# Moving the matmul operands of four stages to other byte addresses in SBUF

## The chip, the core and the metric

The kernel runs on one core of one Trainium2 chip (trn2). The metric is the device time of one execution in microseconds. Three runs of the kernel before gave 2288.55, 2289.33 and 2289.89 us; their median is 2289.33 us. The profile is one further execution, which took 2291.27 us; the span of its instructions is 2289.5 us.

## The reference

One encoder layer is applied to a prompt of 2048 tokens and to 8 sample streams of 16 tokens each (16 tiles of 128 prompt tokens, and one tile of sample tokens). Everything is float32, with a model width of 1024:

```python
qm, km, vm, om, ip, fp, qa, ka, va = split_in(x @ w_in)          # 1024 -> 2824
hm = mlstm_chunkwise(qm, km, vm, logi, logf, C0, n0, m0)          # 4 heads x 128, chunk 64
hm = sigmoid(om) * head_norm(hm)
ha = swa(rope(qa), rope(ka), va, attn_sinks)                      # window 128, 8 q / 2 kv heads x 64
h  = layer_norm(ALPHA * x + concat(hm, ha) @ w_out)               # 1024 -> 1024
u  = h @ w_up                                                     # 1024 -> 2 x 2816
a, g = split(b_conv + causal_conv3(u, w_conv))
y  = layer_norm(ALPHA * h + (silu(g) * a) @ w_down)               # 2816 -> 1024
```

The outputs are y for prompt and samples, the mLSTM states, the last keys and values and the last two rows of u.

## The kernel before

**Four dense stages.** The input projection, the output projection, the up projection and the down projection hold nearly all of the TensorE work. Input, up and down projection use Strassen's scheme: seven products of half-size blocks (numbered 1 to 7 in the code) take the place of eight. The attention and mLSTM work of small matmuls (`Chains`) is woven between the matmuls of the input and output projections.

**Each float32 product is three matmuls.** `split` (L219 to L222) makes of each operand a high part, cast to `float32r` on ScalarE, and a low part, the difference, on VectorE. A product is then high by high, high by low and low by high. The high and low parts stand in SBUF buffers of 1024 or 1536 elements per partition.

**Stationary and moving operand.** A matmul has a stationary operand of 128 columns, which a weight load (LDWEIGHTS, row `PEld` of the profile) brings into the array, and a moving operand of 128 to 512 columns that streams through it (row `PE`). In the profile a matmul is written out<-in, with the moving operand's name first: `dps<-oh,w` streams tokens `oh` against weights `w`, `dps<-w,oh` streams weights against tokens. The load for the next matmul begins when the matmul before it begins to stream, so that in an unbroken run the two read SBUF at the same time.

**Which operand moves.** In the input projection (`i_product`, L721) the model's weights `w` are stationary for the groups g = 0 and 1 and the tokens move, with 256 columns; for g = 2 to 4 it is the other way round. The gates and keys (`i_direct`, L747) stream 264 columns of weights. The output projection (`mm3`, L226 to L228) streams 512 columns of weights against 128 tokens. The up projection (`f_product`, L1895) streams 384 tokens (in the last block of tokens 320) against 128 columns of weights `uw`. The down projection (`product` in `f_downs`, L2103) streams 512 columns of weights `uw` against 128 tokens `fu`.

**Buffers and addresses.** Pools give out their buffers one after the other, from the left or the right end of SBUF. `pad` (L216) takes a buffer of n bytes that nobody uses, to shift what follows. All weight buffers of a pool have one tag with 4 buffers each (`wlo`, `whi`, in `half` and `f_slot`), and two more (`wex`) in the pools `wx1sb` and `wx2sb`. They are 4096 bytes per partition for weights (4352 for the gates), whole multiples of 256, so that every buffer of a stage starts at the same address modulo 256. The token buffers `hh` and `hl` of the up projection come from `f_buf`, which in the pool `fsb` adds 64 elements, so that the down projection can reuse them as `fu` with an offset of 56 elements.

**What sets the order.** TensorE's order is written out by hand; each other engine and DMA queue runs its instructions in the order in which the code records them. Semaphores between engines are derived from reads, writes and buffer reuse.

Of the kernel before, what the change touches and what calls it, by code (L numbers as in the profile page):

```python
# [8 lines left out]
F32 = mybir.dt.float32  # L9
# [5 lines left out]
P = 128  # L15
# [20 lines left out]

WB = 4
WR = 7


IBLOCKS = [[0, 1, 2, 3, 16], [4, 5, 6, 7], [8, 9, 10, 11], [12, 13, 14, 15]]
# [164 lines left out]
class Prog:  # L206
# [23 lines left out]
    def run(self):  # L230
        PS = bass.MemoryType.PSUM
        nb = len(OBLOCKS)
        with ExitStack() as es:
            def enter(*a, **k):
                cm = self.pool(*a, **k)
                return cm.__enter__(), cm
            close = lambda cm: cm.__exit__(None, None, None)
            self.cp = es.enter_context(self.pool("const"))
            self.dp = es.enter_context(self.pool("dram", space=bass.MemoryType.DRAM))
            es.enter_context(self.tc.manual_schedule(engines={mybir.EngineType.PE}))  # L240
            self.setup()
# [12 lines left out]
            wx, wxcm = enter("wx1sb")  # L254
            self.pad(wx, 192)
            self.unit_more(wx)
            self.mp, mcm = enter("osb")
            self.o_setup()
            for b in range(nb - 1):
                chains.weave(self.late_done(self.o_block(b)))  # L260
            chains.until(NPT - 1)
            chains.drain()
            close(tpcm)
            close(tcm)
            self.fp, fcm = enter("fsb", side="right")
            self.fup, fpcm = enter("fup", 3, PS)
            self.f_setup()
            dense = self.o_block(nb - 1)
            first = self.f_hT(0)
            next(first)  # L270
            n = 0
            for i, _ in enumerate(dense):
                if i >= 2:
                    next(first, None)

                if i in (4, 7, 10):
                    self.f_tokens(0, *{4: (1,), 7: ("t1",), 10: ("t3", 7, "t2", 6)}[i])
# [12 lines left out]
            self.pad(self.wx, 192)  # L290
            self.f2, f2cm = enter("f2sb")
            self.pad(self.f2, 64)
            self.f3, f3cm = enter("f3sb")
            self.pad(self.f3, 192)
            self.pad(self.fp, 224)
            self.f_ups(n)
            close(f3cm)
            close(f2cm)
            self.f2, f2cm = enter("d2sb")
            self.f3, f3cm = enter("d3sb")  # L300
            self.f_downs()
            for cm in (f3cm, f2cm, wxcm, fpcm, fcm):
                close(cm)


    def setup(self):
# [3 lines left out]
        nc.vector.memset(self.eps, EPS)  # L310
        self.mhalf = cp.tile([P, 8], F32, name="mhalf")
        nc.vector.memset(self.mhalf, -0.5)
        self.zqk = [dp.tile([8, P, P * len(b)], F32, name=f"zqk{i}") for i, b in enumerate(IBLOCKS)]
        self.zws = [[dp.tile([1 if g < KEPT else 2, P, 4, HT], F32, name=f"zws{g}_{i}") for i in range(4)] for g in range(NG)]
        self.zo = [[dp.tile([len(b), P, 512], F32, name=f"{n}{i}") for i, b in enumerate(IBLOCKS)] for n in ("zqa", "zog", "zv")]
# [79 lines left out]
    def release(self, n):  # L395
        self.halves[1] += n

    def half(self, shape):
        n = self.halves[0]
        self.halves[0] += 1  # L400
        if self.extra is not None:
            e = (n - self.extra) % (2 * WB + 2)
            if e < 2:
                return self.wx.tile(shape, F32R, name="w", tag="wex", bufs=2)
        self.turn = 1 - self.turn
        return self.wp.tile(shape, F32R, name="w", tag=("wlo", "whi")[self.turn], bufs=WB)

    def unit_more(self, wx):
        self.wx, self.extra = wx, self.halves[0]
# [62 lines left out]
    def next_split(self):  # L472
# [7 lines left out]
        self.us += 1  # L480
        if u[0] == "g":
            e = self.raw_of.pop(u)
            w = self.half([P, 2, 2, 272])[:, :, :, :264]
            self.split(w[:, 0], w[:, 1], e[0])
            e[1] = True
            self.wu[u] = w[:, 0], w[:, 1]
            return True
        hi, lo = self.half([P, 1024]), self.half([P, 1024])
        if self.kept(u):
            for i, t in enumerate((hi, lo)):  # L490
                self.nc.sync.dma_start(t.bitcast(F32), self.zws[u[2]][SUMS.index(u[3])][i].rearrange("p a b -> p (a b)"))
# [1212 lines left out]
    def f_hT(self, b):  # L1704
# [12 lines left out]
        if b == 0:  # L1717
# [1 line left out]

            n = len(tiles) // 2  # L1720
            for ts, tags in ((range(n), ("hh6", "hl6")), (range(n, 2 * n), ("hh7", "hl7"))):
                w = [self.f_buf(fp, F32, "hst", tag, [3, 512]) for tag in tags]
# [31 lines left out]
    def f_tokens(self, b, *steps):  # L1754
# [6 lines left out]
        for s in steps:  # L1761
# [7 lines left out]
                V.tensor_sub(r3, r3, r2)  # L1769
            else:  # L1770
                pool = self.fp if s in (1, 7, 6) else self.f3 if s == 4 else self.f2
                hi, lo = [self.f_buf(pool, F32R, f"{n}{s}", f"{n}{s}", [4, 384]) for n in ("hh", "hl")]
                self.split(hi[:, :, :h], lo[:, :, :h], src[s])
                self.hc[b, s] = hi[:, :, :h], lo[:, :, :h]

    def f_buf(self, pool, dt, name, tag, shape, at=0):

        t = pool.tile([P, 1536 + (64 if pool is self.fp else 0)], dt, name=name, tag=tag, bufs=1)[:, at:at + 1536]
        d = dict(zip("abc", shape[:-1]))
        return t.rearrange(f"p ({' '.join(d)} m) -> p {' '.join(d)} m", **d)  # L1780

    def f_slot(self, dt=F32R):
        self.slot = (self.slot + 1) % 10
        if self.slot < 8:
            return self.wp.tile([P, KD, P], dt, name="uw", tag=("whi", "wlo")[self.slot % 2], bufs=WB)
        return self.wx.tile([P, KD, P], dt, name="uw", tag="wex", bufs=2)

    def f_raw(self, b, j):

# [9 lines left out]
    def f_next(self):  # L1799
# [6 lines left out]
        if s == 1:  # L1806
            if (b, j) not in self.wr:
                self.f_raw(b, j)
            if b == 0:
                v, g = self.wr[b, j]  # L1810
                s12, s34 = self.f_slot(F32), self.f_slot(F32)
# [4 lines left out]
                self.wr[b, j] = v, g, s12, s34  # L1816
        if s == 5 and (b, j) != (len(FBLOCKS) - 1, NFF - 1):
            self.f_raw(b + (j + 1) // NFF, (j + 1) % NFF)
        w = self.f_slot().rearrange("p (i k) m -> p i k m", i=2)
        i = SUMS.index(s) if s in SUMS else None  # L1820
        keep = None if i is None else self.zw[j][i].rearrange("p (i k m) -> p i k m", i=2, k=4)
        if b and i is not None:
# [206 lines left out]
    def d_weights(self):  # L2029
# [17 lines left out]
    def d_tokens(self):  # L2047
# [28 lines left out]
    def f_downs(self):  # L2076
# [13 lines left out]
        nb, nu = len(FBLOCKS), len(DUNITS)  # L2090
        ys, ops = {}, {}
        last_tile = FBLOCKS[-1][0]
        st = self.wp.tile([P, 2, 6], F32, name="st", tag="st", bufs=1)

        def product(s, p, units):
# [124 lines left out]
```

## Time and profile before

| | us |
|---|---|
| median of three runs | 2289.33 |
| the profiled execution | 2291.27 |
| its span, first to last instruction | 2289.5 |
| TensorE busy (PE) | 2269.4 |
| weight loads (PEld) | 2083.6 |
| VectorE busy | 1808.9 |
| ScalarE busy | 1272.9 |

Lines such as L721 are lines of the kernel before. A row of groups shows busy time and the mean duration of one instruction. Matmuls overlap each other at their ends, so the time that one costs is the distance between the starts of two that follow each other, which this document calls the period; it is had from the first and the last start and the count. The views by line give each group's least, median and greatest duration, then first and last start. The chain of waits gives start, length, engine, tile, line and count.

### The profile page before, as it was taken

To read this page: it belongs to the slowest core of one execution; us is meant where nothing else is said; L and a number is where in the kernel's file an instruction comes from. 1 tells how busy PE (TensorE), PEld (TensorE's weight loads), DVE (VectorE), ACT (ScalarE), POOL (GpSimd) and SP (SyncE) were. 2 spreads that over 40 slices of the span, in tenths; PEclk is the share of its full clock that TensorE was granted. 3 is DMA by queue.
4 is the path that set the end of the run, shared out by engine and by line. 5 is a ranking of instruction groups with operands and counts; after the bars stand their busy time and mean duration, and the time that the engine had idled before them with its cause. 6 is when DMAs were issued, how large, how long until landed. Compare 5 with 4: busy or idle time off the path is not lost. (4 is left out here: it accounts for less than half of the span.)

```text
span 2289.5 us, 39775 instructions
## 1 busy us (share of the span) xinstructions
PE 2269.4 (99%) x14293; PEld 2083.6 (91%) x14293; DVE 1808.9 (79%) x3068; ACT 1272.9 (56%) x2373; POOL 275.5 (12%) x509
## 2 busy tenths in 40 slices
PE   8999999999999999999999999999999999999998
PEld 8999999999878778999999999999999988888876
DVE  8787687777688888998778777778766786995987
ACT  5453476776766656555556555555555644444442
POOL 0001001000021110211112000113111200200200
PEclk9999999999999999999999999999999999999999
DMA  7989998899998867898778999988998786757752
GB/s 280 321 313 317 319 317 275 276 308 298 329 315 266 270 217 273 310 328 302 285 272 272 307 305 311 307 269 290 323 288 262 253 291 227 252 164 223 251 157 84
DMA packets 302133, 631.30 MB, mean 276 GB/s; under 512 B 47404, under 2 KB 140656, under 8 KB 301936
## 3 DMA queue, kind: packets, MB, share of 16 engines
q1 hardware_dynamic: 297264, 615.06, 79.5%
q0 software_dynamic: 3520, 10.56, 1.5%
q10 hardware_dynamic: 1152, 3.15, 0.4%
q8 instruction: 113, 1.85, 0.3%
q14 instruction: 84, 0.69, 0.1%
HBM read 457.02 MB, written 171.64 MB: 275 GB/s over the span
## 5 line engine op out<-in xcount | busy, mean ns | idle before, releaser
L1895 PE MATMUL fup<-hh,uw 128*128 128x384 f32 (+1 forms) x1848 | 476.9, 327 | 0.2 <-ACT ub L1924 0.2
L1895 PE MATMUL dps<-hh,uw 128*128 128x384 f32 (+1 forms) x1848 | 476.7, 327 | 0.0
L1895 PEld LDWEIGHTS fup<-hh,uw 128*128 128x128 f32 x1848 | 329.1, 188 | 0.5 <-ACT ub L1924 0.4
L1895 PEld LDWEIGHTS dps<-hh,uw 128*128 128x128 f32 x1848 | 329.1, 188 | 0.0
L1895 PE MATMUL fup<-hl,uw 128*128 128x384 f32 (+1 forms) x924 | 301.9, 327 | 1.0 <-DVE hl L222 1.0
L1895 PE MATMUL dps<-hl,uw 128*128 128x384 f32 (+1 forms) x924 | 301.6, 326 | 0.0
L1953 DVE SCALAR_TENSOR_TENSOR cc<-u,cw,cc 128x768 f32<-128x768 f32 (+1 forms) x264 | 258.0, 978 | 38.6 <-ACT cc L1951 30.2
L221 ACT CAST uw<-wraw 128x1024 fp32r<-128x1024 f32 x126 | 123.6, 981 | 229.0 <-PE dps L2103 122.5
L721 PE MATMUL dps<-w,oh 128*128 128x256 f32 x1344 | 250.3, 282 | 0.4 <-ACT dps L815 0.4
L222 DVE TENSOR_TENSOR w<-wraw,w 128x1024 fp32r<-128x1024 f32 (+2 forms) x163 | 186.1, 1149 | 61.8 <-ACT w L221 60.4
L221 ACT CAST w<-wraw 128x1024 fp32r<-128x1024 f32 (+2 forms) x163 | 160.3, 992 | 112.6 <-PE dps L721 58.3
L721 PEld LDWEIGHTS dps<-w,oh 128*128 128x128 f32 x1344 | 209.5, 188 | 11.5 <-issue 8.1
L222 DVE TENSOR_TENSOR uw<-wraw,uw 128x1024 fp32r<-128x1024 f32 x126 | 142.3, 1129 | 61.7 <-ACT uw L221 61.2
L721 PE MATMUL dps<-w,ol 128*128 128x256 f32 x672 | 186.8, 278 | 0.0
L1895 PEld LDWEIGHTS fup<-hl,uw 128*128 128x128 f32 x924 | 173.6, 188 | 1.7 <-DVE hl L222 1.6
L721 PE MATMUL dps<-oh,w 128*128 128x256 f32 x896 | 170.7, 284 | 3.8 <-DVE w L222 2.2
L2103 PE MATMUL fup<-uw,fu 128*128 128x512 f32 x726 | 173.8, 396 | 0.0
L1895 PEld LDWEIGHTS dps<-hl,uw 128*128 128x128 f32 x924 | 173.6, 188 | 0.0
L2103 PEld LDWEIGHTS fup<-uw,fu 128*128 128x128 f32 x726 | 136.4, 188 | 33.0
L2103 PE MATMUL dps<-uw,fu 128*128 128x512 f32 x660 | 165.0, 396 | 0.0
L2103 PEld LDWEIGHTS dps<-uw,fu 128*128 128x128 f32 x660 | 124.0, 188 | 30.0
L721 PEld LDWEIGHTS dps<-oh,w 128*128 128x128 f32 x896 | 140.5, 188 | 10.1 <-issue 4.1
(320 smaller groups left out, 4565.1 us busy)
## 6 DMA issues: line engine op xcount, KB each, us to landing
uw<-zw SPq DMA_DIRECT2D x176, 512.0 KB, 5.1
zw<-uw SPq DMA_DIRECT2D x88, 512.0 KB, 3.3
w<-zws SPq DMA_DIRECT2D x72, 512.0 KB, 6.3
wv<-wup SPq DMA_DIRECT2D x66, 512.0 KB, 5.4
wraw<-wi SPq DMA_DIRECT2D x65, 512.0 KB, 5.1
wraw<-zt SPq DMA_DIRECT2D x60, 512.0 KB, 4.6
wraw<-wdn SPq DMA_DIRECT2D x45, 512.0 KB, 4.9
wraw<-wo SPq DMA_DIRECT2D x40, 512.0 KB, 4.9
```

Of the source, the lines that this page charges most:

```text
L221: nc.scalar.copy(hi, src)
L222: return nc.vector.tensor_sub(lo, src, hi.bitcast(F32)).ins
L721: mm(o, l, r, start=s in (1, 7) and c == k == i == 0, stop=k == 3 and i == 2, skip_group_check=True)
L1895: mm(ps, l[:, k], r[:, k], start=s in (1, 7) and k == 0 and i == 0, stop=k == 3 and i == 2, skip_group_check=True)
L1953: V.scalar_tensor_tensor(c[:, v], u[:, i:i + n], w[i], c[:, v], op0=ALU.mult, op1=ALU.add)
L2103: mm(ps, l[:, k, c], r[:, k], start=s in (1, 4, 7) and u == 0 and k == 0 and i == 0, stop=u == nu - 1 and k == n - 1 and i == 2, skip_grou ...
```

## The change

It shifts buffers and leaves everything else. The order of the instructions on all five engines and what each waits for are the same in both built programs. All weight buffers become 1088 elements (4352 bytes) long, and `half` and `f_slot` return a slice that begins `at` elements into the buffer. The padding is arranged so that weight buffers begin at 0 modulo 256 in every pool, where they began at 192. `f_buf` with its extra elements is gone.

The table gives, from the built programs, how far the stationary operand of the next load lies from the moving operand of the running matmul, in bytes modulo 256 (called the distance below).

| stage, line before | matmuls | columns | moving | next load of | distance before | after |
|---|---|---|---|---|---|---|
| input, g = 0 and 1, L721 | 1344 | 256 | tokens oh, ol | w | 192 | 64 |
| input, g = 2 to 4, L721 | 2016 | 256 | w | oh, ol | 64 | 64 |
| input, samples, L731 | 240 | 256 | w | xs | 96, 128, 192 | 0 to 224 mixed |
| gates and keys, L747 | 408 | 264 | w | oh, ol | 0, 64, 128, 192 | 0, 64, 128, 192 |
| output, L226 to L228 | 816 | 512 | w | oh, ol | 64 | 0 |
| up, L1895 | 3696 | 384 | hh, hl | uw | 192 | 192 |
| up, last block, L1895 | 1848 | 320 | hh, hl | uw | 192 | 192 |
| down, L2103 | 1980 | 512 | uw | fu | 32 | 0 |

In the gates' row a third of the pairs has a distance of 0 before and after; the rest trades 64, 128 and 192 among each other. The operands of the attention and mLSTM matmuls keep their addresses. Raw weights (`wraw`), residual rows (`yacc`) and the raw tokens of the down projection (`r2` to `r4`) move mostly from 192 to 0 modulo 256 with the rest.

```diff
+WS = 1088
...
             wx, wxcm = enter("wx1sb")
-            self.pad(wx, 192)
...
             self.wx, wxcm = enter("wx2sb")
-            self.pad(self.wx, 192)
             self.f2, f2cm = enter("f2sb")
-            self.pad(self.f2, 64)
...
         nc.vector.memset(self.mhalf, -0.5)
+        self.pad(cp, 64)
...
-    def half(self, shape):
+    def half(self, at, size):
...
-                return self.wx.tile(shape, F32R, name="w", tag="wex", bufs=2)
+                return self.wx.tile([P, WS], F32R, name="w", tag="wex", bufs=2)[:, at:at + size]
         self.turn = 1 - self.turn
-        return self.wp.tile(shape, F32R, name="w", tag=("wlo", "whi")[self.turn], bufs=WB)
+        return self.wp.tile([P, WS], F32R, name="w", tag=("wlo", "whi")[self.turn], bufs=WB)[:, at:at + size]
...
-        hi, lo = self.half([P, 1024]), self.half([P, 1024])
+        at = 0 if u[0] == "o" else 16 if u[2] < 2 else 48
+        hi, lo = self.half(at, 1024), self.half(at, 1024)
...
-                hi, lo = [self.f_buf(pool, F32R, f"{n}{s}", f"{n}{s}", [4, 384]) for n in ("hh", "hl")]
+                hi = pool.tile([P, 4, 384], F32R, name=f"hh{s}", tag=f"hh{s}", bufs=1)
+                lo = pool.tile([P, 4, 384], F32R, name=f"hl{s}", tag=f"hl{s}", bufs=1)
...
-    def f_slot(self, dt=F32R):
+    def f_slot(self, at, dt=F32R):
...
+        return w[:, at:at + D].rearrange("p (k m) -> p k m", k=KD)
...
-        w = self.f_slot().rearrange("p (i k) m -> p i k m", i=2)
+        w = self.f_slot(48).rearrange("p (i k) m -> p i k m", i=2)
...
-        hi, lo = [self.f_slot().rearrange("p a b -> p (a b)") for _ in range(2)]
+        hi, lo = [self.f_slot(0).rearrange("p a b -> p (a b)") for _ in range(2)]
...
-        w = self.f_buf(self.fp, F32R, "fu", ("hh1", "hl1", "hh7", "hl7", "hh6", "hl6")[self.ring % 6], [2, 2, 384], 56)
+        w = self.fp.tile([P, 2, 2, 384], F32R, name="fu", tag=("hh1", "hl1", "hh7", "hl7", "hh6", "hl6")[self.ring % 6], bufs=1)
```

More of the change, by code (lines that the diff above doesn't have):

```diff
@@ L482, in next_split @@
             e = self.raw_of.pop(u)
-            w = self.half([P, 2, 2, 272])[:, :, :, :264]
+            w = self.half(0, WS).rearrange("p (i k m) -> p i k m", i=2, k=2)[:, :, :, :264]
             self.split(w[:, 0], w[:, 1], e[0])
@@ L1721, in f_hT @@
             for ts, tags in ((range(n), ("hh6", "hl6")), (range(n, 2 * n), ("hh7", "hl7"))):
-                w = [self.f_buf(fp, F32, "hst", tag, [3, 512]) for tag in tags]
+                w = [fp.tile([P, 3, 512], F32, name="hst", tag=tag, bufs=1) for tag in tags]
                 for c, t in enumerate(ts):
@@ L1771, in f_tokens @@
                 pool = self.fp if s in (1, 7, 6) else self.f3 if s == 4 else self.f2
-                hi, lo = [self.f_buf(pool, F32R, f"{n}{s}", f"{n}{s}", [4, 384]) for n in ("hh", "hl")]
+                hi = pool.tile([P, 4, 384], F32R, name=f"hh{s}", tag=f"hh{s}", bufs=1)
+                lo = pool.tile([P, 4, 384], F32R, name=f"hl{s}", tag=f"hl{s}", bufs=1)
                 self.split(hi[:, :, :h], lo[:, :, :h], src[s])
                 self.hc[b, s] = hi[:, :, :h], lo[:, :, :h]
[L1776 to L1780, printed above, removed]
-    def f_slot(self, dt=F32R):
+    def f_slot(self, at, dt=F32R):
         self.slot = (self.slot + 1) % 10
         if self.slot < 8:
-            return self.wp.tile([P, KD, P], dt, name="uw", tag=("whi", "wlo")[self.slot % 2], bufs=WB)
-        return self.wx.tile([P, KD, P], dt, name="uw", tag="wex", bufs=2)
+            w = self.wp.tile([P, WS], dt, name="uw", tag=("whi", "wlo")[self.slot % 2], bufs=WB)
+        else:
+            w = self.wx.tile([P, WS], dt, name="uw", tag="wex", bufs=2)
+        return w[:, at:at + D].rearrange("p (k m) -> p k m", k=KD)
     def f_raw(self, b, j):
@@ L1810, in f_next @@
                 v, g = self.wr[b, j]
-                s12, s34 = self.f_slot(F32), self.f_slot(F32)
+                s12, s34 = self.f_slot(48, F32), self.f_slot(48, F32)
                 V.tensor_add(s12[:, :4], g[:, :4], g[:, 4:])
@@ L2092, in f_downs @@
         last_tile = FBLOCKS[-1][0]
+        self.pad(self.wp, 192)
         st = self.wp.tile([P, 2, 6], F32, name="st", tag="st", bufs=1)
```

## The prediction

> **What bounds the kernel now.** I read the page's totals first, then TensorE's waits, then single runs of matmuls.
>
> ```profile
> span 2289.5 us, 39775 instructions
> PE 2269.4 (99%) x14293; PEld 2083.6 (91%) x14293; DVE 1808.9 (79%) x3068; ACT 1272.9 (56%) x2373; POOL 275.5 (12%) x509
> PEclk9999999999999999999999999999999999999999
> ...
> PE dps L721 <- DVE w L222: 2.2, 2, 1.3
> PE dps L336 <- DVE zero L331: 2.0, 1, 2.0
> ```
>
> TensorE is busy for 99% of the span, at the full granted clock in all 40 slices, and the longest of its waits for another engine come to 2.2 and 2.0 us in all. Whatever a matmul's period loses or gains is therefore the kernel's, less what the woven work of other engines takes back. By stage (input, output, up, down projection):
>
> ```profile
> 20.00:614.00 594.00, 587.91 (x5048) 558.88 (x5047) 443.76 (x1008) 361.93 (x792) 43.96 (x70) 1.00 0.91 304
> 615.00:894.00 279.00, 278.11 (x1530) 216.93 (x1529) 238.43 (x556) 174.12 (x418) 44.93 (x49) 1.00 0.81 270
> 894.00:1818.00 924.00, 922.83 (x5636) 921.09 (x5635) 727.25 (x977) 519.95 (x879) 155.36 (x355) 1.00 0.86 293
> 1818.00:2281.00 463.00, 462.83 (x1982) 371.56 (x1980) 380.24 (x488) 203.78 (x260) 30.06 (x30) 1.00 0.63 209
> ```
>
> The columns are stage, length, then busy time and count of PE, PEld, VectorE, ScalarE, GpSimd, then clock and DMA share. VectorE comes nearest to TensorE in the output stage, 238 of 279 us; nowhere is there another engine within a few per cent, so a few us saved on TensorE will reach the end.
>
> Since no instruction changes its place or its waits, the only thing that can change is how long one instruction takes at its new addresses. ScalarE, VectorE and the DMA queues, which also get new addresses, have 15% or more to spare in each stage except for the DMA's 0.91 in the first; I cost them at nothing. Were that cover gone in the first stage, transfers that take 1% longer or shorter would move the end by 594 x 0.91 x 1% = 5 us. So the question is the period of a matmul at each distance. A matmul's recorded length overlaps the next, so periods come from starts.
>
> **512 columns, at 64 and 32.**
>
> ```profile
> L227 PE MATMUL dps<-w,oh x25: 393/398/398, 850.5 to 867.3; 128*128 128x512 f32 x25
> 1818.43 46.20 PE fup L2103 x198
> ```
>
> In the output stage L227 is one in three: 16.8 us over 24 steps is 700 ns for three, a period of 233.3 ns at distance 64. The chain of waits has 198 matmuls of the down stage in 46.20 us, 233.3 ns at distance 32. Two distances, one period.
>
> **384 and 320 columns, at 192.** A window of the up stage and a row of the chain:
>
> ```profile
> 920.00:1020.00 100.00, 100.00 (x578) 100.00 (x578) 1.00 0.87 322
> 1784.53 1.76 PE fup L1895 x12
> ```
>
> Less the two that were begun before it, 100 us hold about 576.5 matmuls of 384 columns: 173.4 ns. Twelve of 320 columns take 1.76 us: 146.7 ns. The 64 columns between them cost 26.7 ns, 0.417 each. By that slope 512 columns would take 226.8 ns; they take 233.3, about 6.6 more. Either this step belongs to the length, or to the distance (192 against 32 and 64). This stage keeps its 192, so its 916 us stay.
>
> **256 columns, at 192 and at 64.** Three unbroken runs of the input stage, the first at 192, the others at 64:
>
> ```profile
> L721 PE MATMUL dps<-oh,w x63: 279/279/280, 165.9 to 176.9; 128*128 128x256 f32 x63
> L721 PE MATMUL dps<-ol,w x32: 279/279/279, 165.8 to 176.8; 128*128 128x256 f32 x32
> ...
> L721 PE MATMUL dps<-w,oh x60: 276/276/276, 130.9 to 140.9; 128*128 128x256 f32 x60
> L721 PE MATMUL dps<-w,ol x30: 276/276/276, 130.8 to 140.7; 128*128 128x256 f32 x30
> ...
> L721 PE MATMUL dps<-w,oh x70: 281/281/281, 223.7 to 235.9; 128*128 128x256 f32 x70
> L721 PE MATMUL dps<-w,ol x34: 281/281/281, 224.0 to 235.6; 128*128 128x256 f32 x34
> ```
>
> 95 matmuls from 165.8 to 176.9 are 11.1 us over 94 steps: 118 ns. 90 from 130.8 to 140.9 are 10.1 over 89: 113.5 ns. 104 from 223.7 to 235.9 are 12.2 over 103: 118.4 ns. So a run of matmuls holds one of two paces from its start to its end, about 113.4 or 118, and the recorded length tells which: 276 is the quick pace, 279 (at 192) and 281 (at 64) the slow one. The rows of the whole execution give the shares:
>
> ```profile
> L721 PE MATMUL dps<-w,oh x1344: 276/276/467, 71.6 to 613.6; 128*128 128x256 f32 x192
> L721 PE MATMUL dps<-oh,w x896: 276/279/471, 20.6 to 527.9; 128*128 128x256 f32 x180
> ...
> L721 PE MATMUL dps<-w,ol 128*128 128x256 f32 x672 | 186.8, 278 | 0.0
> L721 PE MATMUL dps<-ol,w 128*128 128x256 f32 x448 | 125.1, 279 | 0.0
> ```
>
> At 64 the median is the quick 276 and the mean of `w,ol` 278 ns, which lies 3/5 of the way from 281 to 276. At 192 median and mean are the slow 279. So at 64 about 60% of the matmuls go at the quick pace, at 192 hardly any.
>
> **The change part by part.**
>
> *Input, g = 0 and 1: 1344 matmuls from 192 to 64.* If they get the other groups' shares, 60% of them gain 118 - 113.4 = 4.6 ns: 1344 x 0.6 x 4.6 = 3.7 us less. Bounds: nothing (no run changes pace), and all of them quick, 1344 x 4.6 = 6.2 us less. The 2016 matmuls of g = 2 to 4 keep their 64, but which pace a run falls into is settled at its start, and starts will shift; should a fifth of them change over, that is 2016 x 0.2 x 4.6 = 1.9 us either way, so I allow 2 us.
>
> *Gates and samples: 648 matmuls.* At L747 all four distances stand side by side before:
>
> ```profile
> L747 PE MATMUL dps<-w,oh x54: 283/283/286, 290.8 to 300.4; 128*128 128x264 f32 x54
> L747 PE MATMUL dps<-w,ol x26: 283/284/285, 291.0 to 300.2; 128*128 128x264 f32 x26
> ```
>
> The least and the median length are alike, so distances of 0 and 64 on one row and 128 and 192 on the other cost the same within 1 or 2 ns. 648 x 1 ns is 0.6 us either way; taken as 0.
>
> *Output and down stage: 816 + 1980 = 2796 matmuls of 512 columns from 64 and 32 to 0.* One ns on each of them is 2.8 us, so this term decides the sign. The trace shows this distance once with this kind of load, where the output stage hands over to the up stage:
>
> ```profile
> 893.77 0.40 PE L228 MATMUL dps<-w,ol 128*128 128x512 f32 x1
> 893.78 0.19 PEld L1884 LDWEIGHTS fup<-hh,uw 128*128 128x128 f32 x1
> 894.01 0.40 PE L1884 MATMUL fup<-hh,uw 128*128 128x512 f32 x1
> ```
>
> The load of `uw` begins 10 ns after the matmul at a distance of 0, and the next matmul starts 0.24 us after it, no sooner than at 64. A second pair of places asks what a load costs at all: the first L228 has no load beside it, the second has the usual one at 64.
>
> ```profile
> 848.13 0.40 PE L228 MATMUL dps<-w,ol 128*128 128x512 f32 x1
> 848.46 0.20 PEld L1367 LDWEIGHTS ppo<-pth,kva 128*64 128x64 f32 x4 [0.36 <-ACT mixm L1198]
> 848.57 0.69 DVE L1629 SCALAR_TENSOR_TENSOR ymix<-ymix,dps 128x512 f32<-128x512 f32 x1 [6.33 <-PE dps L228]
> ...
> 854.93 0.39 PE L228 MATMUL dps<-w,ol 128*128 128x512 f32 x1
> 854.94 0.19 PEld L226 LDWEIGHTS dps<-w,oh 128*128 128x128 f32 x1
> 855.37 0.69 DVE L1629 SCALAR_TENSOR_TENSOR ymix<-ymix,dps 128x512 f32<-128x512 f32 x1 [0.32 <-PE dps L228]
> ```
>
> VectorE, which waits for the result, starts 0.44 us after the first and 0.44 after the second. A matmul of 512 columns that streams alone is done no sooner. So at 64 the load beside it costs nothing that a better distance could give back, and I take the step of 6.6 ns for a matter of length: this term is 0. Bounds: if it were a matter of distance after all, 2796 x 6.6 = 18.5 us less; if distance 0 brings the slow pace that 256 columns show, 2796 x 4.6 = 12.9 us more.
>
> *Sum.* 2291.27 - 3.7 = 2287.6 us for the profiled execution, which stands 1.94 us above the median of the runs; on the runs' scale 2289.33 - 3.7 = 2285.6, and I say 2285.5.
>
> In the Trainium skill, the page "TensorE: Matmul & The Clock Gate", section "Step-by-step: what each phase is for", says that TensorE has two independent read ports into SBUF, so that loading the next tile's weights takes nothing from the running matmul. By that rule no distance can matter and the time would stay at 2289.3. The pair at L228 agrees with it (0.44 us with and without a load); the two paces at L721 do not (113.4 against 118 ns).
>
> **The rivals.**
>
> *Distance 0 frees the 512 columns.* The step of 6.6 ns over the line through 320 and 384 would then be a collision at 32 and 64 that 192 and 0 avoid. For it: at L721 the address does set the pace, and runs lock into paces a few ns apart. Against it: two distances, 32 and 64, with one period; the L228 without a load; the single step at 0. In full it gives 2285.5 - 18.5 = 2267; a third of it, which a pace of two quick in three matmuls or the like would give, 2279.
>
> *Distance 0 is the worst one.* Load and matmul then start in step at the same place of each 256 bytes, 10 ns apart. If runs at 0 fall into a slow pace as those at 192 do with 256 columns, the 2796 matmuls of output and down stage pay up to 4.6 ns: 2285.5 + 12.9 = 2298.4. It decides from 3 ns on (2796 x 3 = 8.4 us, more than the 3.7 gained and the 4.6 of the measurement's resolution together). For it: 192 shows that a distance can cost that. Against it: the step of 0.24 us at 893.77, and the even rows of L747.
>
> *The distance does nothing.* The paces at L721 would belong to the operands' roles (tokens moving at 192, weights moving at 64), which the change leaves. Then the time stays at 2289.3. Against it: both paces occur with the same roles at 64.
>
> **How the numbers follow.** A measurement of this kernel can tell 0.2%, 4.6 us, from no change: below 2284.8 is faster, above 2293.9 slower. My forecast has a chance of 0.45, the freed 512 columns 0.27, the worst distance 0.14, no effect at all 0.14. The forecast's own range is 2281 to 2290: its first term between 0 and 6.2, with 2 us for the other groups' runs. 2285.5 lies close to the border, so about 0.17 of its 0.45 falls to faster and 0.28 to no change. Faster is then 0.17 + 0.26 = 0.43 (a small part of the second case stays within), no change 0.28 + 0.14 + 0.03 = 0.45, and slower 0.12, as a little of the third case stays within too. For 8 in 10 the range goes down to 2270, which takes in most of the second case, and up to 2296, most of the third.
>
> **What would show it.** Right: L721 `dps<-oh,w` with a median of 276, runs of L721 in the g = 0 and 1 stretches at 113 to 114 ns; 198 matmuls of L2103's line in 46.2 us; 576 or so of 384 columns in 100 us as before; the down stage as long as before. If the 512 columns are freed, the same 198 take 44.9 us, and the down stage alone is shorter by up to 13 us. If 0 is the worst, they take 46.8 to 47.1. If the distance does nothing, `dps<-oh,w` keeps its 279. The prediction is wrong as a whole if the up stage's period changes, since nothing there is moved against each other, or if waits of TensorE for DVE or DMA grow beyond a few us.

## The result, and the profile after

Six runs of the changed kernel took 2271.59 to 2274.99 us, median 2272.91; six of the kernel before, on the same chip, 2288.55 to 2291.77, median 2289.61. The ratio is 0.9926, with a 95% interval of 0.9914 to 0.9939: 16.7 us or 0.74% less. The profiled execution after took 2271.59 us, 19.68 less than the one before. Of these, 3.0 us belong to the two executions and not to the change: the one before stands 1.7 us above its median, the one after 1.3 below. One execution of the kernel before took 2773.38 us at a granted clock of 0.75; it is in no median and no ratio here.

Line numbers have shifted a little: L721 stays, the output projection is now L227 to L229, the up projection L1892, the down projection L2101. The page's totals of the changed kernel:

```profile
span 2269.8 us, 39775 instructions
PE 2249.8 (99%) x14293; PEld 2080.5 (92%) x14293; DVE 1807.6 (80%) x3068; ACT 1273.3 (56%) x2373; POOL 273.1 (12%) x509
PEclk9999999999999999999999999999999999999999
```

TensorE's longest waits in it (us in total, times, longest):

```profile
PE dps L721 <- DVE w L223: 2.5, 2, 1.5
PE dps L335 <- DVE zero L330: 2.0, 1, 2.0
```

TensorE is as full as before, at the same clock, and waits as little: its busy time fell by 19.6 us and the span by 19.7. The number of instructions is the same; some of them have become shorter. Which ones, the rows by line of the changed kernel tell (least, median and greatest length, then first and last start):

```profile
L721 PE MATMUL dps<-oh,w x896: 276/276/470, 20.1 to 525.1; 128*128 128x256 f32 x180
L721 PE MATMUL dps<-w,oh x1344: 276/276/467, 70.9 to 610.8; 128*128 128x256 f32 x192
L227 PE MATMUL dps<-w,oh x272: 387/393/504, 612.1 to 886.5; 128*128 128x512 f32 x136
L228 PE MATMUL dps<-w,oh x272: 387/389/402, 612.5 to 886.8; 128*128 128x512 f32 x136
L1892 PE MATMUL fup<-hh,uw x1848: 307/336/421, 887.5 to 1803.7; 128*128 128x384 f32 x124, 128*128 128x320 f32 x61
L2101 PE MATMUL fup<-uw,fu x726: 389/389/395, 1811.4 to 2170.6; 128*128 128x512 f32 x182
```

Rows of the same kind for the kernel before, the ones needed for the stages' borders and the lengths of 512 columns:

```profile
L226 PE MATMUL dps<-w,oh x272: 393/394/505, 615.0 to 893.3; 128*128 128x512 f32 x136
L1895 PE MATMUL fup<-hh,uw x1848: 307/336/423, 894.2 to 1810.6; 128*128 128x384 f32 x124, 128*128 128x320 f32 x61
L2103 PE MATMUL fup<-uw,fu x726: 395/396/396, 1818.3 to 2187.6; 128*128 128x512 f32 x182
```

From the first starts follow the stages' shares. Input, up to the first matmul of the output projection: 615.0 to 612.1, 2.9 us less. Output: 894.2 - 615.0 = 279.2 to 887.5 - 612.1 = 275.4, 3.8 less. Up: 924.1 to 923.9, 0.2 less. Down, to the span's end: 471.2 to 458.4, 12.8 less. Together 19.7. The down stage has two thirds of it, and the chain of waits of the changed kernel shows its period:

```profile
1811.52 44.89 PE fup L2101 x198
1968.80 44.88 PE fup L2101 x198
```

198 matmuls take 44.89 us where they took 46.20: 226.7 ns instead of 233.3. In the output stage, from the starts of consecutive matmuls, the average period went from 233.1 to 229.0 ns; in the input stage's groups g = 0 and 1 from 117.6 to 115.3; the up stage kept 173.3 and 146.7.

### The profile page after: what moved, and what is told of

Its sections match the earlier page's. It is cut to its first block, busy times and chain, and to the rows that moved or that the text cites. A ratio compares the mean times of both kernels' runs of the same rounds, so it can differ in the third digit from the quotient of the medians.

```text
span 2269.8 us, 39775 instructions
## 1 busy us (share of the span) xinstructions
PE 2249.8 (99%) x14293; PEld 2080.5 (92%) x14293; DVE 1807.6 (80%) x3068; ACT 1273.3 (56%) x2373; POOL 273.1 (12%) x509
## 4 chain that ended last, share of the span: by engine, by line
PE 84%; DVE 3%; issue 1%; ACT 1%; DMA 0%; POOL 0%; DVEq 0%; SPq 0%; ACTq 0%; POOLq 0%
PE dps L1892 20%; PE fup L1892 20%; PE dps L721 9%; PE fup L2101 7%; PE dps L2101 7%; PE fht L2101 6%; PE dps L227 3%; PE dps L229 2%; PE dps L228 2%; PE ppo L1367 1%; PE psc L1322 1%; PE ppt L1361 1%; PE dps L747 1%; PE fht L1714 1%; PE pcu L1239 1%
## 5 line engine op out<-in xcount | busy, mean ns | idle before, releaser
L1892 PE MATMUL fup<-hh,uw 128*128 128x384 f32 (+1 forms) x1848 | 476.7, 327 | 0.0
L1892 PE MATMUL dps<-hh,uw 128*128 128x384 f32 (+1 forms) x1848 | 476.5, 327 | 0.0
L1892 PEld LDWEIGHTS fup<-hh,uw 128*128 128x128 f32 x1848 | 329.3, 188 | 0.0
L1892 PEld LDWEIGHTS dps<-hh,uw 128*128 128x128 f32 x1848 | 329.1, 188 | 0.0
L1892 PE MATMUL fup<-hl,uw 128*128 128x384 f32 (+1 forms) x924 | 301.9, 327 | 1.2 <-DVE hl L223 1.2
L1892 PE MATMUL dps<-hl,uw 128*128 128x384 f32 (+1 forms) x924 | 301.7, 327 | 0.0
L721 PE MATMUL dps<-w,oh 128*128 128x256 f32 x1344 | 251.0, 283 | 0.4 <-ACT dps L815 0.4
L721 PEld LDWEIGHTS dps<-w,oh 128*128 128x128 f32 x1344 | 209.7, 188 | 11.5 <-issue 8.1
L721 PE MATMUL dps<-w,ol 128*128 128x256 f32 x672 | 187.0, 278 | 0.0
L1892 PEld LDWEIGHTS fup<-hl,uw 128*128 128x128 f32 x924 | 173.6, 188 | 1.9 <-DVE hl L223 1.8
L1892 PEld LDWEIGHTS dps<-hl,uw 128*128 128x128 f32 x924 | 173.6, 188 | 0.0
L721 PE MATMUL dps<-oh,w 128*128 128x256 f32 x896 | 167.7, 283 | 4.2 <-DVE w L223 2.5
L2101 PE MATMUL fup<-uw,fu 128*128 128x512 f32 x726 | 169.0, 389 | 0.0
L2101 PEld LDWEIGHTS fup<-uw,fu 128*128 128x128 f32 x726 | 136.3, 188 | 28.3
L2101 PE MATMUL dps<-uw,fu 128*128 128x512 f32 x660 | 160.7, 389 | 0.0
L721 PEld LDWEIGHTS dps<-oh,w 128*128 128x128 f32 x896 | 139.9, 188 | 10.4 <-issue 4.1
L2101 PEld LDWEIGHTS dps<-uw,fu 128*128 128x128 f32 x660 | 123.9, 188 | 25.8
```

The lines of the kernel that those rows point to most:

```text
L721: mm(o, l, r, start=s in (1, 7) and c == k == i == 0, stop=k == 3 and i == 2, skip_group_check=True)
L1892: mm(ps, l[:, k], r[:, k], start=s in (1, 7) and k == 0 and i == 0, stop=k == 3 and i == 2, skip_group_check=True)
L2101: mm(ps, l[:, k, c], r[:, k], start=s in (1, 4, 7) and u == 0 and k == 0 and i == 0, stop=u == nu - 1 and k == n - 1 and i == 2, skip_grou ...
```

## The experiments

The kernel before ran on the same chip each time; its medians were 2289.8, 2290.3 and 2289.8 us. The changed kernel had 2272.91 us in its first six runs and 2273.91 in five later ones, so what is read below from two medians is good to about 1 us. Where a period is given without a row, it is the mean of the differences between the starts of consecutive matmuls of a kind in the trace, without those at a pause.

### Down stage alone back at 32

```diff
-        hi, lo = [self.f_slot(0).rearrange("p a b -> p (a b)") for _ in range(2)]
+        hi, lo = [self.f_slot(56).rearrange("p a b -> p (a b)") for _ in range(2)]
```

> The changed kernel with only the down stage's weights moved on by 224 bytes, so that its distance is 32 as before. First theory (distance): 233.3 ns for each of the 1980 matmuls, 198 of them in 46.2 us, and 1980 x 6.6 = 13 us more than the changed kernel: 2286 us, a ratio of 0.998 to the kernel before. Second theory (start address): the same, as the weights move from 224. If the down stage's gain came from the transfers or writes into buffers that now start on 256 bytes, the period stays at 226.7 and the time at 2273 us.

Measured: 2285.58 us (2284.00 to 2286.72, 10 runs), a ratio of 0.998 [0.997, 0.999]. The chain of waits of this kernel:

```profile
1813.92 46.20 PE fup L2101 x198
```

The old period is back with the old distance, and 12.7 of the 16.7 us with it; the periods alone give 13.0. This is the down stage's share; everything else of the change gives some 4 us.

### Input groups g = 0 and 1 alone back at 192

```diff
-        at = 0 if u[0] == "o" else 16 if u[2] < 2 else 48
+        at = 0 if u[0] == "o" else 48 if u[2] < 2 else 48
```

> The changed kernel with only the weights of the input stage's groups 0 and 1 at a distance of 192 from the moving tokens again (1344 matmuls of 256 columns). Distance theory: median length of dps<-oh,w back at 279 ns, a period of 118, and 3 us more than the changed kernel: 2276 us. If these two groups' share of the gain is nothing, 2273 us.

Measured: 2274.65 us (2274.10 to 2275.07, 4 runs), a ratio of 0.9933 [0.9918, 0.9948]. The row of its tokens is the old one again:

```profile
L721 PE MATMUL dps<-oh,w x896: 276/279/471, 19.9 to 527.1; 128*128 128x256 f32 x180
L227 PE MATMUL dps<-w,oh x272: 387/393/504, 614.1 to 889.0; 128*128 128x512 f32 x136
```

The median is 279, and the tokens' period is 117.6 ns again, 1344 x 2.3 = 3.1 us more; the other groups, at 115.0 instead of 115.4 ns, give 0.7 of that back. The output stage starts at 614.1 instead of 612.1 (613.1 in a second execution of the changed kernel, shown below). By the times this part is worth 1.7 us, but their interval overlaps that of the changed kernel, so the times alone do not settle it.

### Output stage alone back at 64

```diff
-        at = 0 if u[0] == "o" else 16 if u[2] < 2 else 48
+        at = 48 if u[0] == "o" else 16 if u[2] < 2 else 48
```

> The changed kernel with only the output stage's weights back at a distance of 64. By the periods (816 matmuls of 512 columns at 229.0 ns in the changed kernel, 233.1 before) 3.4 us slower than the changed kernel: 2276.3, a ratio of 0.9942 to the kernel before. If the gain of the changed kernel is the down stage's alone (12.7 us) and the tokens' (1.7 to 3): 2273 as the changed kernel.

Measured: 2275.30 us (2274.57 to 2275.79, 4 runs), a ratio of 0.9936 [0.9920, 0.9953]. By the medians 2.4 us are lost; the interval overlaps that of the changed kernel, so the times alone do not settle it. The trace does, by its rows by line and then its chain of waits:

```profile
L227 PE MATMUL dps<-w,oh x272: 393/394/505, 612.5 to 889.8; 128*128 128x512 f32 x136
L228 PE MATMUL dps<-w,oh x272: 388/394/398, 612.8 to 890.0; 128*128 128x512 f32 x136
```

```profile
1814.46 44.89 PE fup L2101 x198
```

From the first L227 to the last, the output stage now lasts 2.9 us longer (612.5 to 889.8 against 612.1 to 886.5; 2.2 longer than in the second execution of the changed kernel), its average period is 233.1 ns again, and the down stage keeps 44.89. The three parts put back one by one cost 12.7 + 1.7 + 2.4 = 16.8 us, the whole gain. That the sum comes out so close is luck, as each term is good to about 1 us.

### A map: every stage through 16 distances, twice

In two kernels each stage's weights walk through sixteen offsets, one after the other. In the first the tokens of the down stage stay at 0 modulo 256. In the second the order is another, and `pad(fp, 64)` moves those tokens (and some of the up stage's) to 224, so that the same distance occurs at other addresses.

```diff
+DSCAN = [0, 8, 16, 24, 32, 40, 48, 56, 4, 12, 20, 28, 36, 44, 52, 60, 0, 32, 48, 16, 56]
...
-        hi, lo = [self.f_slot(0).rearrange("p a b -> p (a b)") for _ in range(2)]
+        at = DSCAN[7 * b + (DLAST if b == len(FBLOCKS) - 1 else DORDER).index(s)]
+        hi, lo = [self.f_slot(at).rearrange("p a b -> p (a b)") for _ in range(2)]
```

> A map in one execution: the weights' slices begin at 16 different byte offsets in turn (0 to 240 modulo 256, in steps of 16), another one for each product of the down stage, for each few units of the input and up stages and for each group of the output stage. Tokens stay where the changed kernel has them (0 modulo 256), so the distance runs through all its values. Nothing is left out. First theory (the distance sets the period): matmuls of 512 columns take 226.7 ns at distance 0 and 233.3 at 32 and 64; 256 columns go quick (113.4) in part of the runs at 64 and hardly ever at 192; 384 and 320 columns take 173.3 and 146.7 at 192; the values between are not known and are what the run is for. Second theory (the start address of the moving operand sets it: quick when it starts on a multiple of 256): in the down stage the moving weights are quick at 0 alone and at 233.3 at most other offsets; in the up stage and in the input stage's first two groups, where the tokens move and stay at 0, one period at all 16 offsets. The total time says nothing here.

> The same map with the offsets in another order, and with the buffers of one pool shifted, so that the tokens of the down stage and of three of the up stage's seven products begin at 224 modulo 256 instead of 0. Nothing is left out. First theory (distance): each distance has the period that it has in the map without the shift; 512 columns of weights that move from 224, at distance 0, take 226.7 ns, and those that move from 0, at distance 224, take whatever distance 224 took in the first map. Second theory (start address of the moving operand): weights that move from 0 take 226.7 ns at distance 224 as well, and those from 224 take 233.3 at distance 0. If a run keeps the pace that it began with (a third theory: the pace is handed on from matmul to matmul, whatever the address), the periods follow the order of the offsets and not the offsets, and the two maps do not agree.

Measured: 2294.69 and 2297.44 us (one run each), slower than before, since most distances are poor. The periods in ns, first kernel / second kernel, for twelve of the sixteen distances (96, 112, 176 and 208 show nothing else):

| distance | 512, down | 384, up | 320, up | 256, tokens move | 256, weights move |
|---|---|---|---|---|---|
| 0 | **226.7 / 226.9** | 173.3 / 173.6 | 146.6 / 146.7 | 119.9 / 119.8 | 119.9 / 119.9 |
| 16 | 233.3 / 233.3 | 173.3 / 173.7 | 146.7 / 146.7 | 118.3 / 118.3 | 117.2 / 117.2 |
| 32 | 233.3 / 233.3 | 173.4 / 173.6 | 146.7 / 146.8 | 118.3 / 118.1 | 118.2 / 118.3 |
| 48 | 234.7 / 234.7 | 173.3 / 173.4 | 144.7 / 146.2 | 118.2 / 120.5 | 118.7 / 119.2 |
| 64 | 233.3 / 233.3 | 173.9 / 175.2 | 146.6 / 146.7 | 117.8 / 114.9 | **115.8 / 113.6** |
| 80 | 233.3 / 233.3 | 176.0 / 176.0 | 146.6 / 145.8 | 118.8 / 118.6 | 119.2 / 119.3 |
| 128 | 232.8 / 232.4 | 176.0 / 175.8 | 146.7 / 146.7 | 118.9 / 118.9 | 118.6 / 118.8 |
| 144 | 231.3 / 231.2 | 173.5 / 175.5 | 146.6 / 146.6 | 119.4 / 119.9 | 114.5 / 115.9 |
| 160 | 233.4 / 233.4 | 176.7 / 176.7 | 146.6 / 146.7 | 120.1 / 120.0 | 120.0 / 120.0 |
| 192 | 228.9 / 228.9 | **173.3 / 173.3** | **146.6 / 146.7** | 117.7 / 117.8 | 117.8 / 116.4 |
| 224 | 233.3 / 233.3 | 173.6 / 174.5 | 146.7 / 146.7 | 116.7 / 117.1 | 116.9 / 116.9 |
| 240 | 231.6 / 231.7 | 174.1 / 176.7 | 146.7 / 146.6 | 118.0 / 118.1 | 114.6 / 117.2 |

Rows of the first kernel: distance 0 with moving weights at 0, then 224 with them at 32, then 32 with them at 224, and in the last two 144 with them at 112.

```profile
L2116 PE MATMUL fup<-uw,fu x99: 389/389/398, 1824.0 to 1846.3; 128*128 128x512 f32 x99
L2116 PE MATMUL fup<-uw,fu x101: 389/394/399, 1846.0 to 1869.4; 128*128 128x512 f32 x101
L2116 PE MATMUL fup<-uw,fu x99: 392/395/397, 1984.7 to 2007.5; 128*128 128x512 f32 x99
L2116 PE MATMUL fht<-uw,fu x66: 387/392/401, 2076.7 to 2098.6; 128*128 128x512 f32 x66
L2116 PE MATMUL dps<-uw,fu x34: 387/392/398, 2076.4 to 2099.3; 128*128 128x512 f32 x34
```

Rows of the second kernel: distance 0 with moving weights at 224, then 224 with them at 0.

```profile
L2117 PE MATMUL fup<-uw,fu x99: 389/389/397, 1987.3 to 2009.5; 128*128 128x512 f32 x99
L2117 PE MATMUL dps<-uw,fu x67: 393/394/397, 1963.9 to 1987.0; 128*128 128x512 f32 x67
```

Weights that begin at 224 have the quick length of 389 ns in the second kernel (distance 0) and 395 in the first (distance 32); weights that begin at 0 have 394 in the second (distance 224) and 389 in the first (distance 0). The distance decides here, not where the moving operand begins, nor where the stationary one does (in the second kernel it begins at 224 both with 226.9 and with 233.3 ns). For 512 columns the two kernels agree within 0.4 ns at each distance. Nor is it that VectorE and ScalarE write into slices that begin on 256 bytes, since in the second kernel the quick slices begin at 224. For 512 columns 0 is the best of the sixteen; 16 bytes to one side cost the whole step (233.3), 16 to the other most of it (231.6). 384 columns have their floor of 173.3 at several distances and up to 3.4 ns more at others, 320 columns hardly mind these sixteen, and 256 columns have no distance at which both roles are quick.

For 384 and 256 columns the distance alone does not set the period. At 240 the two kernels have 174.1 and 176.7 ns for 384 columns; at 64, with moving tokens of 256 columns, 117.8 and 114.9; the 117.8 is no better than the same kernel's 117.7 at 192. What else counts there was not found.

### The low parts of the weights alone at another distance

```diff
-        hi, lo = [self.f_slot(0).rearrange("p a b -> p (a b)") for _ in range(2)]
+        hi, lo = [self.f_slot(at).rearrange("p a b -> p (a b)") for at in (0, 48)]
```

> The changed kernel, but in the down stage the low parts of the weights begin 192 bytes further on. Of the 1980 matmuls of 512 columns, which come in triples high by high, high by low, low by high, 1320 keep a distance of 0 and every third (660) goes to 64. If each matmul's own pair of addresses sets its period: two at 226.7 ns and one at 233.3, on average 228.9, so 198 matmuls in 45.3 us, the stage 4.4 us longer than in the changed kernel, about 2277.3 in all. If a run of matmuls shares one pace, set by its slowest member: 233.3 for all, 198 in 46.2 us, about 2286. If it is shared and the majority sets it: 226.7 for all, 2272.9.

Measured: 2279.46 us (one run). The chain of waits:

```profile
1815.24 45.34 PE fup L2101 x198
1973.95 45.32 PE fup L2101 x198
```

45.32 us are 228.9 ns for one, just what two at 226.7 and one at 233.3 give. The stage became 4.2 us longer (the sum of its periods, 453.9 against 449.7). The odd pair neither slows the whole run nor is it swallowed: its price of 6.6 ns is paid in full, once per triple. Within the triple it is not seen at its own place: the three members have 228.3, 229.3 and 229.2 ns, so the matmuls' starts spread it over their neighbours. The total is 2.2 us above the 2277.3 that were expected; that lies ahead of the down stage and is within what single executions vary by.

### Which pair: the operand held, or the operand being loaded?

```diff
+FS = 1552
...
-        w = self.fp.tile([P, 2, 2, 384], F32R, name="fu", tag=("hh1", "hl1", "hh7", "hl7", "hh6", "hl6")[self.ring % 6], bufs=1)
+        w = self.fp.tile([P, FS], F32R, name="fu", tag=("hh1", "hl1", "hh7", "hl7", "hh6", "hl6")[self.ring % 6], bufs=1)
+        w = [w[:, at:at + 768].rearrange("p (k m) -> p k m", k=2) for at in (0, 784)]
...
```

> The changed kernel, but the low parts of the down stage's tokens begin 64 bytes later in a longer buffer, so that successive token buffers begin at 0, 64, 128 and 192 modulo 256. The moving weights stay at 0. A matmul's own stationary operand and the one that is loaded beside it then lie at different distances: of 1980 matmuls 420 have the next load at 0, 360 at 64, 600 at 128 and 600 at 192, with the own stationary operand spread about evenly in each group. If the load beside the matmul sets its period (read access against read access): 226.7, 233.3, 232.6 and 228.9 ns in these four groups whatever the own operand, on average 230.4, the stage 7.2 us longer than in the changed kernel. If the own operand, loaded before, sets it: the same four figures sorted by the own operand and no difference by the next. If a run shares one pace: no difference by either. The up stage's tokens share these buffers, so a third of its matmuls leave 192 for 64, 128 and 0; by the map 384 columns then cost up to 3 ns more at 128, about 2 us in all. Total 2280 to 2284.

Measured: 2280.62 us (one run), the down stage 7.7 us longer than in the changed kernel (457.4 against 449.7), where 7.2 had been worked out from the map's prices. The sum is right, and the total lies in the range expected; the sorting was not what either theory expects:

| distance | 0 | 64 | 128 | 192 |
|---|---|---|---|---|
| by the map | 226.7 | 233.3 | 232.6 | 228.9 |
| sorted by the next load | 230.4 | 231.3 | 231.8 | 229.8 |
| sorted by the operand held | 228.4 | 233.2 | 231.5 | 230.4 |

Sorted by the operand held, the order is the map's, though less far apart. But that operand is the one which was loaded beside the matmul before, and the experiment above shows that a matmul's price turns up at its neighbours' starts. So this is also what one would see if the load sets the price and the start after next shows it. Nor does the operand held set the period alone: with it at 64, the period is 235.8 ns where the next load is at 0 and 228.8 where that is at 128. Which of the two reads is in the way stays open.

### A fine map

The same walk, in steps of 4 to 12 bytes around the good distances (lists of offsets in the place of `DSCAN` and its like).

> A map in steps of 4 to 12 bytes around the best distances, each stage's weights going through a list of offsets: 512 columns around 0, 192, 180 and 144, 384 columns around 0, 50, 110 and 192, 320 columns from 36 to 88, 256 columns around 64, 144 and 244. If the period depends on which 16-byte piece of the 256 bytes the two reads are in, 4 to 12 bytes off 0 keep 226.7 ns and 233.3 begins at 16. If it depends on both reads being aligned, 4 bytes off 0 already cost 233.3. Around 64, 256 columns either hold one pace of 113.4 ns at some neighbour (then there is a better offset than the changed kernel's 64, worth up to 3360 x 1.9 ns = 6 us), or keep two paces. The 384 columns stay at 173.3 and the 320 at 146.6 or above. The total tells nothing, as most offsets are poor ones: 2285 to 2300.

Measured: 2302.78 us (one run), a little above the range expected. Rows of this kernel: 512 columns at distance 4, at 252, at 188 (two rows) and at 144.

```profile
L2118 PE MATMUL fup<-uw,fu x101: 387/388/395, 1855.0 to 1877.8; 128*128 128x512 f32 x101
L2118 PE MATMUL fht<-uw,fu x66: 390/399/405, 1924.8 to 1947.4; 128*128 128x512 f32 x66
L2118 PE MATMUL fht<-uw,fu x66: 391/403/403, 2062.1 to 2084.9; 128*128 128x512 f32 x66
L2118 PE MATMUL dps<-uw,fu x33: 403/403/403, 2065.0 to 2085.6; 128*128 128x512 f32 x33
L2118 PE MATMUL fup<-uw,fu x101: 388/389/396, 2177.3 to 2199.9; 128*128 128x512 f32 x101
```

99 matmuls at 188 lie between 2062.1 and 2085.6: 239.8 ns. The periods around 0 are 226.8 at 0, 228.8 at 4, 233.4 at 8, 239 at 12, and on the other side 237.2 at 252, 232.3 at 248, 228.9 at 244. So neither theory holds: there is no piece of 16 bytes within which the distance does not matter, and being off by 4 bytes on one side costs 2 ns, on the other 10. The last row is the surprise: 144, with the weights at 112, has 226.7 ns here and 231.2 in the first map, at the same addresses. What differs is the product and its PSUM tiles (`fup` here, `fht` and `dps` there) and what ran ahead. Some distances have more than one pace. At 0 all long runs of 512 columns in the kernels here had 226.7 to 227.1.

For 256 columns the fine map had one offset with only quick matmuls where tokens move: 113.1 and 114.0 ns at 76, 82 matmuls in all. 64 with moving weights had 113.3, with moving tokens 117.8. For 384 columns the lowest is 173.1, the floor again, but at 40 they take 179.7. And 320 columns, which hardly minded the sixteen distances of the first maps, take 148.3 ns at 76, 149.7 at 60 and 152.4 at 84.

### A better offset for the tokens' weights?

```diff
-        at = 0 if u[0] == "o" else 16 if u[2] < 2 else 48
+        at = 0 if u[0] == "o" else 19 if u[2] < 2 else 48
```

> The changed kernel, but the weights of the groups g = 0 and 1 of the input stage begin at 76 instead of 64. In the fine map 82 matmuls of 256 columns at this distance had 113.1 and 114.0 ns, all at the quick pace; in the changed kernel the 1344 of these groups average about 115.3. If the distance alone sets the pace: 1344 x 1.9 = 2.6 us less than the changed kernel, 2270.3. If a run falls into a pace by how it starts, and the 82 were two lucky runs: as the changed kernel within 1 us, or up to 1344 x 4 = 5 us slower, as the moving weights at 76 were (121 ns).

> The changed kernel itself, on the same chip as the version with 76: 2272.9, a ratio of 0.9926 to the kernel before. It says whether a difference of 2.6 us between the two is theirs.

Measured, on one chip: 2271.09 us with 76 (2269.52 to 2272.07, 5 runs), 2273.91 for the changed kernel itself (2272.58 to 2274.64, 5 runs). The two ranges do not touch; the difference of 2.8 us is 0.12%. Their ratios to the kernel before are 0.9918 [0.9905, 0.9932] and 0.9930 [0.9918, 0.9943], whose intervals overlap. First the row with 76, then in a fence of its own that of the changed kernel:

```profile
L227 PE MATMUL dps<-w,oh x272: 387/393/504, 611.0 to 885.9; 128*128 128x512 f32 x136
```

```profile
L227 PE MATMUL dps<-w,oh x272: 387/393/504, 613.1 to 888.2; 128*128 128x512 f32 x136
```

The output stage starts 2.1 us earlier. The trace shows fewer of the tokens' matmuls at the slow pace, not none: about 80% have 113 or 114 ns (58% at 64), nearly all others 118 to 122. The mean falls from 115.3 to 114.5 ns, 1344 x 0.8 = 1.1 us. That is less than the 2.6 expected of the distance alone; the rest of the 2.1 us lies in pauses and in other matmuls of the input stage and is within what these vary by (the changed kernel's own two profiled executions have their first L227 at 612.1 and 613.1). So the two quick runs of the fine map were in part luck. This version has the lowest median here, if by little.

## Why the prediction was right or wrong

The time lies in the wide range of 2270 to 2296 and on the predicted side, but outside the forecast's own 2281 to 2290: the likeliest case, 2285.5, was wrong, and the wide range held because it was drawn to take in a rival. What came is the rival "distance 0 frees the 512 columns", which had a chance of 0.27 and was given 2267 in full and 2279 for a third.

**TensorE sets the end: right.** 19.6 us less of busy TensorE are 19.7 us less of span; no wait grew by more than about a microsecond, so the costs set at nothing (other engines, the DMA) do not show. By the periods, which are worked out below, the change is worth 13.0 + 3.4 + 3.1 - 0.7 = 18.8 us, by the medians 16.7. The gap is no more than what pauses vary by: two executions of the changed kernel, 2271.59 and 2273.59 us, have the same periods within 0.2 ns.

**The up stage stays: right.** A window of the changed kernel's up stage, beside the 578 of before:

```profile
920.00:1020.00 100.00, 100.00 (x579) 100.00 (x578) 1.00 0.86 321
```

**Input, g = 0 and 1: the mechanism right, the size a little too large.** The median of `dps<-oh,w` went to 276 and about 58% of the tokens' matmuls to the quick pace, as foreseen. That it is the other groups' share is luck in part, as the first map's kernel had 117.8 ns at the same 64. 3.7 us were forecast. The periods give 1344 x 2.3 = 3.1, the part put back costs 1.7 to 2. As allowed for, the other groups moved a little, without a change at their own: 2016 x 0.34 = 0.7 us more.

**Output and down stage: the term of 0 was wrong, by 16.4 us.** The down stage gave 1980 x 6.6 = 13.0 us, its bound in full. The output stage gave 816 x 4.1 = 3.4 of at most 5.4. The prediction had the right number in hand: the slope between 320 and 384 columns led to 226.8 ns, and 226.7 is what 512 columns take at 0. The step that failed is the one behind it, "I take the step of 6.6 ns for a matter of length", and it rested on two readings. A third spoke against the rival "0 is the worst".

*The pair at L228.* It was to show that the load beside a matmul costs nothing, so that no distance could give anything back. It was read at 10 ns in search of 6.6. Read to the ns, from the kernel before:

```profile
L228 PE MATMUL dps<-w,ol x1: 397/397/397, 848.1 to 848.1; 128*128 128x512 f32 x1
L228 PE MATMUL dps<-w,ol x1: 393/393/393, 854.9 to 854.9; 128*128 128x512 f32 x1
```

The first streams alone, and is recorded as longer, not shorter, than the second with its load. And a matmul that streams alone has more than one length. These three of the changed kernel all stand before a pause, the next load 0.32 to 0.33 us after their start:

```profile
L229 PE MATMUL dps<-w,ol x1: 389/389/389, 743.7 to 743.7; 128*128 128x512 f32 x1
L229 PE MATMUL dps<-w,ol x1: 397/397/397, 776.7 to 776.7; 128*128 128x512 f32 x1
L229 PE MATMUL dps<-w,ol x1: 397/397/397, 842.2 to 842.2; 128*128 128x512 f32 x1
```

389 and 397 ns with no load beside them: something other than the load sets the recorded length of a single matmul, perhaps what ran ahead of it, which is not shown. A lone one is therefore no floor against which to price a load. Only long runs are, and the prediction had none at 0.

*The single step at 0.* 0.24 us for one matmul between two others of another kind says nothing of the pace of a run. The output stage after has such steps too, 224 to 240 ns in the first few matmuls after each pause, before it settles at 226.7. This is why it averages 229.0 and gave 3.4 us and not 5.4.

*The even rows of L747.* They gave the gates a term of 0, which was right: their average period went from 121.8 to 121.2 ns, 0.2 us. But the rows could not tell what a distance costs. They are even in length; from start to start the same stretch goes through 120 to 124 ns in a pattern of twelve. The row `dps<-w,oh` holds all four distances, `dps<-w,ol` 0 and 64, and the distance changes from one matmul to the next. In such a mixture the starts spread a price over the neighbours, as the experiment with the low parts shows.

**"Two distances, one period": a fair reading that misled.** Of the sixteen distances in the map, eight have 233.1 to 233.4 ns. 32 and 64 are two of them; that they agree was likely even if the distance mattered.

**Rival "0 is the worst": refuted for 512, true for 256.** 256 columns have 119.8 ns at 0, among the slowest of their column. What this rival carried over from them to 512 columns does not carry over: each length has its own good distances.

**Rival "the distance does nothing": refuted.** The Trainium skill, "TensorE: Matmul & The Clock Gate", section "Step-by-step: what each phase is for", gives the stationary and the moving operand a read port each, from which the prediction concluded that no distance could matter. The trace does not agree with that conclusion: 226.7 and 233.3 ns with nothing changed but where the operands lie.

## What to carry to other kernels

Where TensorE is full, compare the period of long unbroken runs with the line through the other lengths (here 0.417 ns for a column): for an excess, try the addresses before putting it down to the length; a walk of one operand through the offsets modulo 256 answers it in one run. The best distance belongs to the shape: 0 for 512 columns, 64 or 76 for 256, 192 among others for 384, and moving an operand by 16 bytes can cost 3% of a stage. Don't price a steady stream from single instructions, whose length varied here by 8 ns with no load beside them, nor a distance from a run that mixes several.

## What was not expected of the hardware

**Paces come in steps.** In units of 0.417 ns, the time of one column, the steady periods exceed the number of columns by 16 (113.3 for 256), by 32 (146.7 for 320, 173.3 for 384, 226.7 for 512), by 48 (233.3) or by 64 (240.0 at a distance of 140). Other averages lie between them where the three matmuls of a triple differ, such as 226, 229 and 232 ns, on average 229, for 512 columns at 192.

**The dependence is fine and not symmetric.** From 0, 4 bytes cost 2 ns on one side and 10 on the other; 188 has 239.8 ns and 192 has 228.9.

**One address, several paces.** Distance 144 with 512 columns had 231.2 and 226.7 ns, and 64 with 256 columns has both paces in every kernel. What picks the pace as a run starts was not found, nor which of the two reads is held up.
